# Two row buffers in an expert loop, the last tile's rows added by a product, and three smaller reorderings, in a two-layer backbone

## The chip, the cores and the metric

One Trainium2 chip, one of its cores. The metric is the device time of one execution of the program, in microseconds (us). The kernel before was timed in three runs.

## The reference, cut to what matters

Two layers run over 256 latent tokens and 256 context tokens of width 1024. Each layer mixes tokens (a state space branch, a gated branch, differential attention, sigmoid gates, one output projection) and then sends every token through 8 of 64 experts and one shared expert. All is float32. In the last layer only the latent tokens go through the experts.

```python
# differential attention, per head: two score matrices, m = 0 and 1
s = einsum('bqhmd,bkhmd->bhmqk', q, k) * DA_HEAD_DIM ** -0.5
p = softmax(s); attn = p[:, :, 0] - lam * p[:, :, 1]
...
out = m @ w_out                                    # the out product of the mixer
h = layer_norm(DN_ALPHA * h + g1 * out, ln1_g, ln1_b)
f = modulate(layer_norm(h), sh2, sc2)
...
# experts: each token's rows through its 8 experts, weighted, summed over the experts
yb = swiglu(h_pad[tok], w_gate[e], w_up[e], w_down[e]) * wt[:, None]
y = segment_sum(yb, row_tok) + swiglu(h, w_sh_gate, w_sh_up, w_sh_down)
h = layer_norm(DN_ALPHA * h + g2 * y, ln2_g, ln2_b)
```

## The kernel before, in words

Outside the expert stage a list scheduler orders the instructions of each engine, with a cost model; `self.urgent`, `self.hold`, `background` and `paced` are hints to it. Inside `experts` (from line 1521) the order is written by hand.

**Expert stage.** The (token, expert) pairs are sorted by expert into tiles of 128 rows, made of four groups of 32 rows, each with one expert. The groups belong to three lanes, `LANE_OF = (0, 0, 1, 2)`, so that a token appears at most once per lane and tile; each lane has an accumulator in DRAM, `acc`, of one row of 1024 numbers per token. Layer 0 has 38 tiles and layer 1 has 20; the first 32 and 16 are always run, the rest stand in nested conditions (`rest`, line 1684). One step `body(t)` issues, in this order: the gate and up products of tile t (`gate_up`, line 1630, 64 records on the product engine); the last weight copies of the tile; the activation; the transposes of tile t+1's gathered rows (`x_t`); the weight copies of tile t+1 from the ring of loaded weights (`copy_gu`, line 1578, lanes 0 and 2 on DVE, lane 1 on ACT; `copy_dn`, line 1584, DVE); the transposes of the hidden rows; POOL's indirect gather of tile t+2's rows (line 1554); and then `down(t-1)`: the down products (line 1646), ACT's two copies of the result, scaled by the routing weight, to the row buffer `Y` (line 1648), with two of ACT's weight copies in between, and POOL's indirect DMA that adds the rows of `Y` to `acc` (the scatter, line 1651).

`Y` is one buffer of 128 x 1024 numbers, so ACT writes tile t's rows once the scatter of tile t-1 has landed. Two scatters add to the same `acc`, so POOL starts one when the one before has landed. ACT runs its instructions in order: what waits for `Y` holds up the weight copies behind it, for which `gate_up` waits. On POOL a gather stands behind the scatter issued before it. SP loads the experts' weights, three times 1 MB each, to a ring of four slots (`load_next`), when DVE's and ACT's copies have freed a slot.

**Combine** (from line 1711). After the last scatter, g2 and the gain and bias of the norm are spread from one row to 128 partitions by products with a row of ones (lines 1719 to 1726) and used from PSUM (the bias is copied to SBUF). Per token tile (four in layer 0, two in layer 1) SP loads the three lanes of `acc` (line 1742); they are added by DVE for the first tile and by POOL for the others (line 1745); DVE multiplies by g2 (line 1746) and adds the scaled residual (line 1748); `ln_two` normalises (DVE, ACT, POOL); SP writes the tile out (line 1752). In layer 0 the next layer's `mixer_input` (lines 330 to 371) follows directly: transposes on the product engine (line 366), then the input projection.

**Attention** (line 731 and on). Per token tile and head, for m = 0 and then m = 1: a score product over 64 rows of the array (line 737), the maximum on DVE (line 740), the exponential on ACT. The two m use different halves of the rows and different PSUM banks.

**Out product, layer 1.** Two token tiles (2 and 3), two halves of 512 columns. The weights of half 1 are prepared ahead by `out_weights`; those of half 0 are loaded and split within a loop over k, which runs tile 2's two halves and tile 3's first half; tile 3's second half follows. Then `residual` (lines 997 to 1000) loads a half of the residual input `op_h` on SP and adds it, `ln_two` runs twice per tile, and the router's products and a sigmoid (line 1042) follow.

The program is made in `kernel` with the default space for the descriptors of indirect DMAs.

## Time and profile before

| | us |
|---|---|
| runs before, median of 3 (lowest to highest) | 2016.36 (2011.74 to 2021.05) |
| the profiled execution, its own time | 2016.54 |
| its span, first to last instruction | 2014.5 |
| around the span | 2.0 |
| mean granted clock of the product engine, share of full speed | 0.921 |

Engines are PE (products; PEld its weight loads), DVE, ACT, POOL and SP (which issues loads); a "q" behind a name is an engine's instruction queue. In a row of the timeline stand the start, the busy time, the engine, the line of the kernel, the operation, what it writes and reads, how many instructions were merged, and in brackets how long the engine stood idle before it and what ended that. A row of the waits says which instruction waited for which, for how long in all, how often, and the longest. [...] Busy shares are averages over stages that have different limits.

### The profile page before, as it was taken

How to read it: one execution, taken by the hardware profiler on the slowest of the kernel's cores; microseconds unless marked ns; L12 is line 12 of the kernel's file. 1: busy time of each engine (PE TensorE's matmuls, PEld its weight loads, DVE VectorE, ACT ScalarE, POOL GpSimd, SP SyncE). 2: the span in 40 equal slices, each digit the busy share in tenths (PEclk: the TensorE clock that was granted, in tenths of full speed). 3: DMA queues.
4: the chain of work that ended last, by engine and by line, in shares of the span. 5: the costliest groups of instructions: out<-in, count | busy, mean ns of one | idle time of the engine just before them, and what ended most of it. 6: DMA issues, size and time to landing. Idle time of an engine off the chain costs nothing. (4 is left out here: it accounts for less than half of the span.)

```text
span 2014.5 us, 33549 instructions
## 1 busy us (share of the span) xinstructions
PE 1724.2 (86%) x12397; PEld 1009.1 (50%) x12397; DVE 1153.1 (57%) x2295; ACT 792.6 (39%) x1317; POOL 585.0 (29%) x385
## 2 busy tenths in 40 slices
PE   5898999999997988999889763889989689897883
PEld 2686866778865323333323221777779653232231
DVE  7688554333654756766565546663554456655554
ACT  3344343323313544555444343432454224443441
POOL 5355310222201324343233224323042202331222
PEclk8898999999998989999999885889999789998996
DMA  8113524553767555677798937635564567999974
GB/s 273 48 48 116 170 95 139 182 191 134 265 240 309 171 187 182 220 220 242 263 354 313 360 90 269 215 130 183 187 194 130 206 245 275 323 343 354 386 263 122
DMA packets 158391, 435.02 MB, mean 216 GB/s; under 512 B 25813, under 2 KB 82547, under 8 KB 133114
## 3 DMA queue, kind: packets, MB, share of 16 engines
q1 hardware_dynamic: 124716, 344.04, 46.5%
q0 software_dynamic: 17280, 51.93, 10.7%
q10 hardware_dynamic: 16206, 36.66, 5.0%
q8 instruction: 103, 1.69, 0.3%
q14 instruction: 86, 0.70, 0.1%
HBM read 403.16 MB, written 55.03 MB: 227 GB/s over the span
## 5 line engine op out<-in xcount | busy, mean ns | idle before, releaser
L1630 PE MATMUL pg<-gu,xt 128*32 128x512 f32 x3712 | 487.4, 641 | 105.0 <-ACT gu L1578 65.8
L1578 DVE COPY gu<-raw 128x1024 f32 x476 | 298.8, 689 | 160.0 <-issue 82.1
L1651 POOL DMA_INDIRECT acc<-y,t_scatter x58 | 208.8, 3600 | 584.0 <-ACT y L1648 313.1
L1630 PEld LDWEIGHTS pg<-gu,xt 128*32 128x32 f32 x3712 | 141.1, 117 | 438.9 <-issue 238.8
L1578 ACT COPY gu<-raw 128x1024 f32 x238 | 244.3, 1043 | 63.2 <-PE pg L1630 35.7
L1646 PE MATMUL py<-dn,ht 128*32 128x512 f32 x1856 | 211.1, 595 | 2.5 <-ACT gu L1578 1.7
L1584 DVE COPY dn<-raw 128x2048 f32 x178 | 212.9, 1224 | 0.4 <-issue 0.4
L136 PE MATMUL mm<-uh,whi 128*128 128x512 f32 (+1 forms) x544 | 199.3, 366 | 7.9 <-ACT rx L849 4.5
L138 PE MATMUL mm<-uh,wlo 128*128 128x512 f32 (+1 forms) x544 | 194.8, 358 | 0.5 <-DVE wlo L315 0.5
L137 PE MATMUL mm<-ul,whi 128*128 128x512 f32 (+1 forms) x544 | 194.2, 357 | 0.0
L315 DVE TENSOR_TENSOR wlo<-raw,whi 128x1024 fp32r<-128x1024 f32 x77 | 97.0, 1261 | 110.6 <-ACT whi L312 110.2
L312 ACT CAST whi<-raw 128x1024 fp32r<-128x1024 f32 x92 | 96.1, 1047 | 145.3 <-PE mm L137 121.3
L1648 ACT ACTIVATE y<-py,w 128x512 f32<-128x512 f32 x116 | 79.7, 689 | 157.0 <-DMA acc<-y,t_scatter 147.5
L1635 DVE TENSOR_TENSOR sg<-sg,pg 128x256 f32<-128x256 f32 x58 | 24.4, 421 | 195.7 <-ACT sg L1634 195.7
L136 PEld LDWEIGHTS mm<-uh,whi 128*128 128x128 f32 x544 | 106.3, 195 | 33.5 <-issue 8.0
L1634 ACT ACTIVATE sg<-pg 128x256 f32<-128x256 f32 x58 | 22.3, 384 | 250.1 <-PE pg L1630 250.1
L137 PEld LDWEIGHTS mm<-ul,whi 128*128 128x128 f32 x544 | 106.3, 195 | 17.1 <-issue 4.6
L1554 POOL DMA_INDIRECT xg<-f,t_gather x62 | 67.3, 1085 | 162.8 <-DVE t_scatter L1518 68.2
L138 PEld LDWEIGHTS mm<-uh,wlo 128*128 128x128 f32 x544 | 106.1, 195 | 16.1 <-issue 2.3
L1646 PEld LDWEIGHTS py<-dn,ht 128*32 128x32 f32 x1856 | 54.6, 109 | 114.9 <-issue 107.9
L1622 PEld LDWEIGHTS px<-ct,xg 128*128 128x128 f32 x480 | 58.8, 194 | 60.1 <-issue 60.1
L1622 PE MATMUL px<-ct,xg 128*128 128x128 f32 x480 | 70.4, 290 | 9.9 <-DMA xg<-f,t_gather 9.9
(482 smaller groups left out, 2823.1 us busy)
## 6 DMA issues: line engine op xcount, KB each, us to landing
raw<-in_w_exp_gate_dram SPq DMA_DIRECT2D x68, 1024.0 KB
raw<-in_w_exp_up_dram SPq DMA_DIRECT2D x68, 1024.0 KB
raw<-in_w_exp_down_dram SPq DMA_DIRECT2D x68, 1024.0 KB
raw<-in_w_in_dram SPq DMA_DIRECT2D x42, 1024.0 KB
mraw<-in_w_mod_dram SPq DMA_DIRECT2D x80, 512.0 KB
cb_y<-acc SPq DMA_DIRECT2D x18, 512.0 KB
fraw<-in_w_mod_dram SPq DMA_DIRECT2D x16, 512.0 KB
acc<-zt ACTq DMA_DIRECT2D x12, 512.0 KB
```

Of the source, the lines that this page charges most:

```text
L136: nc.tensor.matmul(out, lh, rh, start=start, stop=False)
L137: nc.tensor.matmul(out, lh, rl, start=False, stop=False)
L138: self.last = nc.tensor.matmul(out, ll, rh, start=False, stop=stop).ins
L312: self.nc.scalar.copy(hv, src)
L315: i = eng.tensor_tensor(lv, src, hv.bitcast(F32), op=ALU.subtract)
L1578: c = nc.scalar.copy(dst, gu) if ln == 1 else V.tensor_copy(dst, gu)
L1584: c = V.tensor_copy(DN[ln][t % 2].rearrange("p a b -> p (a b)"), srcs[ln][:, 4096:6144])
L1622: nc.tensor.transpose(pX[hf][:, k * P:(k + 1) * P], XG[t % AHEAD][:, 4 * hf + k:D:8], ident)
L1630: nc.tensor.matmul(pG[t % 2][r, :], XT[:, k, r], GU[ln][(4 * t + k // 2) % 3][:, k % 2].rearrange("p g n -> p (g n)"), start=(k == 0), sto ...
L1646: nc.tensor.matmul(pY[hf][r, :], HT[t % 2][:, k, r], DN[ln][t % 2][:, k, 512 * hf:512 * hf + 512], start=(k == 0), stop=(k == 1), tile_pos ...
L1648: nc.scalar.activation(Y[:, 512 * hf:512 * hf + 512], pY[hf], AF.Copy, scale=W[t % 4])
L1651: nc.gpsimd.indirect_dma_start(out=acc, out_offset=bass.IndirectOffsetOnAxis(ap=tb["scatter"][:, t:t + 1], axis=0), in_=Y, in_offset=None, ...
```

## The change

The last expert tile's rows go to a buffer that stays (`self.yl`), with their token numbers (`self.il`); no scatter follows. In `combine` they are added by a product with a 0/1 matrix (token number of the row equal to the column's), accumulated in PSUM with the three lanes, each multiplied by the identity. So the sums of lanes are eight products per token tile, and DVE reads the sum from PSUM. The spread rows are copied to SBUF by ACT, those of the norm after the first tile's products; all tiles of h are loaded at the start. `Y` has two buffers. The space for descriptors of indirect DMAs is set to 8192, half of before. In attention both score products of a head are issued ahead of both maxima. In layer 1 the out product has both halves' weights prepared ahead, runs by tile (tile 2's halves, then tile 3's), the residual input is loaded whole and early, and a sigmoid of one column is issued ahead of the first tile's norm.

```diff
 # attention
-                for m in range(2):
+                both = [pp.tile([P, 512], F32, name="att", tag="att", bufs=2) for m in range(2)]
+                for m, ps in enumerate(both):
                     r = slice(64 * m, 64 * m + 64)
-                    ps = pp.tile([P, 512], F32, name="att", tag="att", bufs=2)
                     qk = nc.tensor.matmul(ps[:, :nk], ...)
+                for m, ps in enumerate(both):
                     mx = pool.tile([P, 1], F32, name="mx", bufs=4)
...
 # out_first
+            if l == DEPTH - 1:
+                half["h"][t] = pool.tile([P, D], F32, name="op_h%d" % t)
+                self.nc.sync.dma_start(half["h"][t], h_tiles[t])
 # out_proj
+            if l == DEPTH - 1 and t == tiles[0]:
+                nc.scalar.activation(pool.tile([P, 1], F32, name="op_sg"), half["sm"][t][:, 0:1], AF.Sigmoid)
 # mixer
+                if not full:
+                    w0 = [ow.tile([P, KC, 512], F32R, name="wn%d" % i) for i in range(2)]
+                    self.out_weights(l, 0, self.mod_raw, *w0)
                 self.out_weights(l, 1, self.mod_raw, *w1)
...
+                for t in tiles if not full else ():
+                    c = slice(t * P - t0, t * P - t0 + P)
+                    for p, w, hf in ((ps[t], w0, 0), (ps1[t], w1, 1)):
+                        self.out_half(p, mh, ml, *w, c.start)
+                        if hf == 0:
+                            self.residual(op, half, t, 0, p, h_tiles[t])
-                for k in range(KC):
+                for k in range(KC) if full else ():
...
 # experts
-            Y = pool.tile([P, D], F32, name="y")
+            Y = [pool.tile([P, D], F32, name="y%d" % i) for i in range(2)]
...
-            def down(t, between=()):
+            def down(t, between=(), last=False):
+                y = self.yl if last else Y[t % 2]
...
-                    nc.scalar.activation(Y[:, 512 * hf:512 * hf + 512], pY[hf], AF.Copy, scale=W[t % 4])
+                    nc.scalar.activation(y[:, 512 * hf:512 * hf + 512], pY[hf], AF.Copy, scale=W[t % 4])
...
+                if last:
+                    V.tensor_copy(self.il, tb["gather"][:, t:t + 1])
+                    return
                 nc.gpsimd.indirect_dma_start(out=acc, ..., in_=y, ..., compute_op=ALU.add)
...
-                        down(t - 1)
+                        down(t - 1, last=True)
...
 # combine
-                return ps
+                v = pool.tile([P, D], F32, name="cb_" + name)
+                nc.scalar.copy(v, ps)
+                return v
...
-            for t in range(2):
+            for t in range(len(streams)):
                 nc.sync.dma_start(tiles[t], h1_tiles[t])
...
-                ys = [pool.tile([P, D], F32, name="cb_y%d" % i, bufs=4 if i < 2 else 2) for i in range(LANES)]
+                ys = [pool.tile([P, D], F32, name="cb_y%d" % i, bufs=3) for i in range(LANES)]
...
-                for a in ys[1:]:
-                    (G if t else V).tensor_tensor(y, y, a, op=ALU.add)
-                V.tensor_mul(y, y, g2[s])
+                if s not in g2:
+                    g2[s] = spread(self.modD[l][s:s + 1, 3 * D:4 * D], "g2_%d" % s)
+                oh = pool.tile([P, P], F32, name="cb_oh", bufs=2)
+                V.tensor_scalar(oh, self.C("iota"), float(t * P), self.il, op0=ALU.add, op1=ALU.is_equal)
+                yp = pp.tile([P, D], F32, name="cb_yp", bufs=2)
+                for i in range(0, D, 512):
+                    for j, (a, w) in enumerate([(self.yl, oh)] + [(a, self.C("ident")) for a in ys]):
+                        nc.tensor.matmul(yp[:, i:i + 512], w, a[:, i:i + 512], start=(j == 0), stop=(j == LANES))
+                if t == 0:
+                    lg, lb = (spread(A[nm][l:l + 1, :], nm) for nm in ("ln2_g", "ln2_b"))
+                y = ys[0]
+                V.tensor_mul(y, yp, g2[s])
...
 # kernel
-    nc = _bacc.Bacc("TRN2", target_bir_lowering=False, num_devices=1)
+    nc = _bacc.Bacc("TRN2", target_bir_lowering=False, num_devices=1, dynamic_dma_scratch_size=8192)
```

## Rows read from the trace of the kernel before

**Rows 1.** The page's part 1: engine, busy us (share of the span) and instructions.
```profile
PE 1724.2 (86%) x12397; PEld 1009.1 (50%) x12397; DVE 1153.1 (57%) x2295; ACT 792.6 (39%) x1317; POOL 585.0 (29%) x385
```

**Rows 2.** The waits, whole span: who waited for whom, us in total, times, longest.
```profile
POOL acc L1651 <- DVE gu L1578: 229.8, 22, 17.3
...
ACT y L1648 <- DMA acc<-y,t_scatter: 147.5, 33, 8.7
```

**Rows 3.** Timeline of PE, a tile that nothing holds.
```profile
867.16 7.05 PE L1630 MATMUL pg<-gu,xt 128*32 128x512 f32 x64
...
879.06 7.05 PE L1630 MATMUL pg<-gu,xt 128*32 128x512 f32 x64
```

**Rows 4.** Timeline of POOL and ACT, a held tile, layer 0.
```profile
692.54 6.03 POOL L1651 DMA_INDIRECT acc<-y,t_scatter  x1 [7.74 <-DVE gu L1578]
...
708.51 0.69 ACT L1648 ACTIVATE y<-py,w 128x512 f32<-128x512 f32 x1 [6.92 <-DMA acc<-y,t_scatter]
...
711.00 1.59 POOL L1651 DMA_INDIRECT acc<-y,t_scatter  x1 [11.08 <-ACT y L1648]
712.89 1.04 POOL L1554 DMA_INDIRECT xg<-f,t_gather  x1 [0.30 <-issue]
```

**Rows 5.** Line 1648's idle time (us, times) in 660 to 880, 880 to 1140, 1680 to 1830.
```profile
  DMA acc<-y,t_scatter: 30.2, 8
...
  DMA acc<-y,t_scatter: 49.3, 11
...
  DMA acc<-y,t_scatter: 32.7, 7
```

**Rows 6.** Stretches: length, busy time by engine, granted clock, DMA share, GB/s.
```profile
667.00:872.00 205.00, 187.82 (x1528) 66.60 (x1523) 129.29 (x201) 99.48 (x143) 77.58 (x30) 0.95 0.64 206
872.00:1132.00 260.00, 232.37 (x1892) 81.51 (x1886) 157.99 (x249) 122.59 (x178) 83.12 (x35) 0.96 0.82 290
...
1204.00:1266.00 62.00, 22.23 (x44) 9.76 (x44) 38.58 (x61) 20.61 (x30) 28.47 (x20) 0.50 0.70 247
...
1686.00:1821.00 135.00, 118.31 (x970) 41.67 (x966) 84.64 (x131) 62.02 (x91) 44.02 (x19) 0.96 0.90 324
...
1860.00:1940.00 80.00, 64.63 (x506) 21.46 (x498) 40.13 (x63) 34.01 (x49) 19.68 (x10) 0.96 1.01 390
```

**Rows 7.** Tile acc, all its 58 scatters and the accumulator loads: time to landing.
```profile
DMA to landing us min/median/max: 5.9/10.7/16.3
```

**Rows 8.** Tile xg, its 62 gathers: time to landing.
```profile
DMA to landing us min/median/max: 4.4/10.2/13.1
```

**Rows 9.** Timeline of all engines at the end of layer 0.
```profile
1206.46 1.27 ACT L1648 ACTIVATE y<-py,w 128x512 f32<-128x512 f32 x2 [8.74 <-DMA acc<-y,t_scatter]
...
1210.61 7.19 PE L1725 MATMUL g<-g,cb_one 1*128 1x512 f32 x8 [11.37 <-POOL cb_one L1717]
...
1216.60 15.28 SPq L1742 DMA_DIRECT2D cb_y<-acc  x12
...
1222.07 2.48 DVE L1745 TENSOR_TENSOR cb_y<-cb_y,cb_y 128x1024 f32<-128x1024 f32 x2 [22.70 <-DMA cb_y<-acc]
...
1225.92 3.40 DVE L1748 SCALAR_TENSOR_TENSOR cb_h<-cb_h,cb_y 128x1024 f32<-128x1024 f32 x1
```

**Rows 10.** Timeline of ACT at the end of layer 1.
```profile
1976.81 1.27 ACT L1648 ACTIVATE y<-py,w 128x512 f32<-128x512 f32 x2 [7.25 <-DMA acc<-y,t_scatter]
```

**Rows 11.** Timeline of PE, DVE and ACT behind layer 1's out product.
```profile
1584.27 0.39 PE L138 MATMUL opp<-whi,mh 128*128 128x512 f32 x1
...
1591.31 0.69 DVE L1000 SCALAR_TENSOR_TENSOR op_r<-op_h,op_r 128x512 f32<-128x512 f32 x1 [3.47 <-DMA op_h<-h]
...
1606.03 1.28 ACT L1042 ACT_TABLE_LOAD   x1 [2.05 <-DVE op_f L189]
```

**Rows 12.** Timeline of PE, score products of layer 1, apart and together.
```profile
1390.34 1.12 PE L737 MATMUL att<-kT,qT 64*128 64x512 f32 x2
...
1395.54 1.13 PE L737 MATMUL att<-kT,qT 64*128 64x512 f32 x4
```

More of the change, by code (lines that the diff above doesn't have):

```diff
@@ L111, in __init__ @@
         self.eps = self.per.tile([P, 3], F32, name="eps")
+        self.yl = self.per.tile([P, D], F32, name="yl")
+        self.il = self.per.tile([P, 1], F32, name="il")
         self.hpi = self.eps[:, 2:3]
@@ L980, in shared_expert, with out_first @@
             yield
-    def out_first(self, l, pool, tiles):
-        half = dict(r={}, sm={}, g={})
+    def out_first(self, l, pool, tiles, h_tiles):
+        half = dict(r={}, sm={}, g={}, h={})
         for s in sorted(set(t // 2 for t in tiles)):
@@ L995, in residual @@
         c = slice(512 * hf, 512 * hf + 512)
-        h = pool.tile([P, 512], F32, name="op_h", bufs=2 if self.l < DEPTH - 1 else 4)
-        self.nc.sync.dma_start(h, h_tile[:, c])
+        if t in half["h"]:
+            h = half["h"][t][:, c]
+        else:
+            h = pool.tile([P, 512], F32, name="op_h", bufs=2)
+            self.nc.sync.dma_start(h, h_tile[:, c])
         r = half["r"][t][:, c]
@@ L1150, in mixer @@
                 op = pool("opr", hx, side="right")
-                half = self.out_first(l, op, tiles)
+                half = self.out_first(l, op, tiles, h_tiles)
                 ow = pool("opw", hx, side="right")
                 w1 = [ow.tile([P, KC, 512], F32R, name="wo%d" % i) for i in range(2)]
+                if not full:
+                    w0 = [ow.tile([P, KC, 512], F32R, name="wn%d" % i) for i in range(2)]
+                    self.out_weights(l, 0, self.mod_raw, *w0)
                 self.out_weights(l, 1, self.mod_raw, *w1)
@@ L1167, in mixer @@
                         self.mm3(ps[t], mh[:, k, c], ml[:, k, c], hv[:, k % 2, :], lv[:, k % 2, :], k == 0, k == KC - 1)
-                        if t == 2 and not full:
-                            self.mm3(ps1[t], mh[:, k, c], ml[:, k, c], w1[0][:, k, :], w1[1][:, k, :], k == 0, k == KC - 1)
-                if not full:
-                    self.out_half(ps1[3], mh, ml, *w1, 3 * P - t0)
-                for t in tiles:
+                for t in tiles if full else ():
                     self.residual(op, half, t, 0, ps[t], h_tiles[t])
@@ L1689, in rest @@
                     with more.Else():
-                        down(t - 1)
+                        down(t - 1, last=True)
                 else:
-                    down(t - 1)
+                    down(t - 1, last=True)
             for t in range(AHEAD):
@@ L1719, in spread @@
             def spread(row, name):
[L1721 removed]
+                v = pool.tile([1, D], F32, name="cb_row", bufs=2)
                 nc.scalar.dma_start(v, row)
[L1723 removed]
+                ps = pp.tile([P, D], F32, name="cb_ps", bufs=2)
                 for i in range(0, D, 512):
                     nc.tensor.matmul(ps[:, i:i + 512], one, v[:, i:i + 512], start=True, stop=True)
[L1726 to L1730 removed]
+                v = pool.tile([P, D], F32, name="cb_" + name)
+                nc.scalar.copy(v, ps)
+                return v
+            g2 = {}
             tiles = [pool.tile([P, D], F32, name="cb_h%d" % t) for t in range(len(streams))]
[L1732 removed]
+            for t in range(len(streams)):
                 nc.sync.dma_start(tiles[t], h1_tiles[t])
```

11 lines of the change are left out of this document (1 added, 10 removed).

## The prediction

> **What bounds the kernel now.** I read the page first, then the waits, then one tile of the expert stage in order of time, then the stages. The page gives the product engine 1724.2 us, 86% of the span [rows 1]. The remaining 290 us are idle time, and after idle time the engine also runs slowly, so the question is which wait holds it up in the expert stages. In the list of waits, two entries belong to one loop: ACT waited 147.5 us, 33 times, for the landing of a scatter before it could write the next y, and POOL's scatter started late behind DVE's weight copies, 229.8 us in 22 waits [rows 2]. The loop exists because y is one buffer: y(t) can't be written until scatter(t-1) has read it and landed.
>
> Two tiles show what the loop costs. A tile that nothing holds takes 879.06 - 867.16 = 11.9 us from one gate/up start to the next [rows 3]. In a held one [rows 4] a scatter issued at 692.54 occupied POOL for 6.03 us, and landed just ahead of 708.51, 16 us after issue. ACT sat 6.92 us, and the weight copies for which gate/up waits stood behind it. The next scatter came at 711.00, 18.46 us after the first: 6.56 us over 11.9, for 6.92 us of waiting. So a wait of y costs the tile 0.95 of its length, partly hidden, and partly paid again in slow products behind the gap.
>
> By stretch, y waited 30.2, 49.3 and 32.7 us [rows 5] (layer 0 early, layer 0 late, layer 1 early; 16, 18 and 10 tiles, at two copies of y each). The other 35.3 us of the 147.5 lie in tiles that wait for weight loads anyway, and in the two last tiles. The loads' own share of the DMA engines was 0.64, 0.82 and 0.90 in these stretches, and 1.01 where loads bind, late in layer 1 [rows 6].
>
> **The row buffers.** With Y in two buffers, y(t) waits for scatter(t-2). Times 0.95 the three stretches could give back 28.7, 46.8 and 31.0 us, which is the upper bound, 106. Two things take from it. First, scatter(t) still waits on POOL for scatter(t-1)'s landing, since both add into one accumulator. Landings took 5.9 / 10.7 / 16.3 us (min, median, max) [rows 7]. Spread evenly over the upper half, 0.39 of the tiles lie above 11.9, by 2.2 us on the mean: 0.87 us a tile is kept. Second, the same bytes must be loaded in less time; at a share of 0.94 (between 0.90 and 1.01) the stretches of 205, 260 and 135 us can't fall below 140, 227 and 129, a gain of at most 33 in the second and 6 in the third, or 13 at a share of 1.0.
> - Early layer 0, 16 tiles: 28.7 - 14 = 15.
> - Late layer 0, 18 tiles: 46.8 - 15.7 = 31, under the limit of 33.
> - Early layer 1, 10 tiles: 31 - 8.7 = 22, limited to 6 to 13, say 9.
> - The late tiles: 0.
>
> The sum is **-55**. With no tile kept and loads at 1.0 it is 28.7 + 46.8 + 13 = -88. If every scatter comes in the upper half (middle 13.5, so 1.6 kept a tile), it is 3 + 18 + 9 = -30. Behind a waiting scatter POOL's next gather is queued. Its landing takes 10.2 us at the median [rows 8] and it is wanted about 11.9 + 7.05 us after y is written, so a scatter that is up to about 6 us late hides it; I count nothing, and a rival counts it.
>
> The scatter's length has a cause in the rows. It is 6.03 us on POOL beside DVE's copies and 1.59 us once they are done [rows 4]. [...]
>
> **Layer 0's end.** The last y waits 8.74 us for the scatter before it; then comes its own scatter, and the accumulator loads issue at 1216.60 [rows 9]. Without the last scatter they can issue when the last y starts now, at 1206.46: 10.1 us earlier. Against that stand the sums by products. [...] I take 9.5 for the first tile, slow at first, less the 2.48 us of DVE adds that go [rows 9]: -10.1 + 9.5 - 2.5 = -3. The three other tiles' products lie beside the normalisation of the tile before, as POOL's adds do now; the scaled add drops from 3.40 us beside those adds [rows 9], so another -2: **-5**. [...] The spreads' copies on ACT and the early loads of h lie beside the wait for the accumulators.
>
> **Layer 1's end.** The last y waits 7.25 us [rows 10], the path is the same and the gain again 10.1. Only two token tiles follow, and nothing after them: -3 for the first, and for the second 7 us of products where about 5 us of the first's normalisation cover, +2: **-1**. [...]
>
> About the clock, the trace shows 0.50 through both the wait and the spreads, from 1204 to 1266 [rows 6]. [...]
>
> **Layer 1's out product.** The last product starts at 1584.27, but a residual half waits until 1591.31 for its load of h, 3.47 us of it idle [rows 11]; a table load of 1.28 us stands ahead of the router's sigmoid. With h loaded early and tile 2 finished half the products sooner, only tile 3's chain is left behind the last product. I take 3.5 for the load, 1.3 for the table and 3 for tile 2's instructions that no longer stand in tile 3's way: **-8** (0 to -11). The extra weights' loads replace as many bytes; their cover is the stage's earlier products.
>
> **Paired scores.** Two score products apart take 1.12 us for two records each; four records together take 1.13 [rows 12]. I counted all 24 pairs: 16 run apart now, so at most 16 x 1 = 16 us; but the engine has other work there while DVE takes the maxima, and order changes elsewhere: **-4** (0 to -15).
>
> **Half the descriptor space:** 0. A scatter at 711.00 and a gather at 712.89 are in flight together [rows 4]; half the space holds at least one.
>
> The sum is -55 - 5 - 1 - 8 - 4 = -73. The profiled execution took 2016.5 us (span 2014.5, 2.0 around it), the median of the runs is 2016.4, so no correction: **1943**.
>
> **Rivals.**
> 1. *Scatters in a chain.* Every scatter takes the long form, and the loop runs at its landing. For it: 22 waits behind DVE [rows 2]. Against: the median of 10.7 is below 11.9. The gain is 30 in place of 55: 1968.
> 2. *Tiles at 11.9 until loads bind.* For it: a gather and a scatter cost nothing in an unheld tile. -88: 1943 - 33 = 1910.
> [...]
> 4. *A gather queued behind a waiting scatter* comes late by what y no longer waits, so the expert stages gain nothing: 1998. It decides once a scatter issues over about 6 us late in two tiles running.
> 5. *Slower: the halved descriptor space holds only one indirect DMA.* Then scatter and gather wait for each other's landing, 10.7 + 10.2 = 20.9 us a tile where I expect 12.8: 58 x 8.1 = 470 us, 2413. It decides as soon as one scatter with one gather exceeds the half; against it is only that the whole holds both.
>
> **Numbers.** My forecast has 0.45, the rivals 0.17, 0.12, 0.12, 0.08 and 0.03, and other losses 0.03. The range reaches from below rival 2 to above rival 3, **1902 to 1990**. A measurement of this kernel can tell about 0.5%, 10 us. Faster: the first four cases and a quarter of rival 4, 0.88. Same: the rest of it, 0.06. Slower: 0.06.
>
> **What would show it.** Right: ACT's wait for the scatter falls from 147.5 to under 50 us, in its place POOL waits for landings; tiles run near 12.8; the accumulator loads issue about 10 us after the last down product's predecessor landed, not 20; the granted clock rises within the sums. [...] The prediction is wrong if the expert stages gain under 30 us or over 88.

## The result, and where the time went

The changed kernel takes 1982.78 us (median of 4 runs, 1978.30 to 1985.32) beside 2015.56 us for the kernel before on the same chip (4 runs, 2011.74 to 2021.05): a ratio of 0.9833, interval [0.9803, 0.9862]. It is faster by 1.7%, and inside the range, but by 33 us where 73 were forecast. The span fell from 2014.5 to 1980.1 us, by 34.4. Ratios here and below are of fast runs; one slow run of E14, at 3302 us, is not in its ratio.

Both traces are cut at the same landmarks (the first gate/up product, the last down product, the first and last score product of layer 1, the last out product, the router's transposes), with the two best experiments beside them. Lengths in us:

| stage | before | changed | difference | E1: rows alone | E10: best |
|---|---|---|---|---|---|
| start to first gate/up product | 641.7 | 646.8 | +5.1 | 647.7 | 647.7 |
| experts, layer 0, to the end of the last down product | 557.5 | 509.6 | **-47.9** | 508.3 | 516.6 |
| layer 0's combine and layer 1's projection, to the first score product | 191.1 | 201.1 | **+10.0** | 173.5 | 172.9 |
| attention, layer 1 | 72.3 | 71.2 | -1.1 | 72.4 | 72.5 |
| last score product to last out product | 121.7 | 134.9 | **+13.2** | 121.7 | 121.5 |
| to the last router transpose | 23.1 | 18.7 | -4.4 | 23.0 | 19.5 |
| to layer 1's first gate/up product | 49.1 | 48.3 | -0.8 | 47.7 | 48.6 |
| experts, layer 1 | 315.2 | 304.6 | **-10.6** | 303.5 | 303.3 |
| combine, layer 1 | 42.8 | 44.9 | +2.1 | 38.0 | 38.2 |
| span | 2014.5 | 1980.1 | -34.4 | 1935.9 | 1940.9 |

So the expert stages gained 58.5 us, and other stages gave 24 of it back. Stages with the same work in them tell how far one profile can be trusted: the first, where only the paired scores and the use of SBUF differ, lies between 641.7 and 648.2 in the runs below, and layer 0's expert stage between 508.3 and 519.0 in those with two row buffers.

The page's part 1 of the changed kernel answers to [rows 1]; the product engine is busier in a shorter span, and POOL less busy:

```profile
PE 1750.4 (88%) x12493; PEld 1026.8 (52%) x12493; DVE 1149.7 (58%) x2300; ACT 803.3 (41%) x1327; POOL 542.0 (27%) x378
```

**The expert stages.** The waits of the changed kernel (who waited for whom, us in total, times, longest) answer to [rows 2]:

```profile
POOL acc L1674 <- DVE gu L1597: 254.0, 26, 17.4
...
POOL acc L1674 <- DMA acc<-y,t_scatter: 63.4, 7, 9.6
...
PEld px L1641 <- DMA xg<-f,t_gather: 36.0, 19, 3.6
...
DVE cb_y L1775 <- PE cb_yp L1771: 28.6, 4, 24.8
```

ACT's wait for the scatter, 147.5 us before, is in the list no more. POOL waits 63.4 us for landings in its place, as the prediction said, and 254.0 behind DVE, but ACT isn't queued behind POOL. The windows of the same stages (length, busy time of PE, PEld, DVE, ACT, POOL, granted clock, DMA share, GB/s), and below them three short ones for later, answer to [rows 6]:

```profile
647.00:847.00 200.00, 193.98 (x1664) 72.03 (x1664) 141.64 (x220) 110.71 (x158) 74.09 (x30) 1.00 0.69 219
847.00:1068.00 221.00, 208.29 (x1806) 75.71 (x1798) 152.78 (x238) 120.48 (x173) 68.56 (x34) 0.99 0.90 314
1631.00:1764.00 133.00, 121.64 (x1036) 45.43 (x1032) 89.80 (x142) 69.30 (x99) 37.66 (x18) 0.97 0.89 333
1764.00:1918.00 154.00, 123.50 (x954) 43.63 (x950) 81.16 (x127) 63.28 (x90) 30.12 (x18) 0.91 0.96 362
...
1160.79:1177.85 17.06, 15.15 (x17) 5.34 (x18) 0.00 (x0) 2.02 (x2) 0.19 (x1) 0.50 0.92 363
...
1939.02:1956.09 17.07, 14.51 (x16) 5.01 (x17) 0.00 (x0) 2.02 (x2) 0.19 (x1) 0.50 0.59 226
...
1528.00:1564.00 36.00, 27.35 (x96) 20.53 (x96) 16.04 (x18) 10.22 (x18) 11.18 (x8) 0.81 0.59 223
```

The first 16 tiles of layer 0 take 12.5 us each (14.1 before), the next 17 take 13.0 (14.2), the first 10 of layer 1 13.3 (14.5); the last 9, where weight loads bind (a DMA share of 0.96 in the fourth window), are no shorter (154.5 us for 152.6). PE works 97% of the first window, and the loads' share rose to 0.90 in the second.

**Layer 0's combine.** The timeline of all engines (start, busy time, what it does, in brackets the idle time before it and its end) answers to [rows 9]:

```profile
1161.00 21.42 SPq L1761 DMA_DIRECT2D cb_y<-acc  x11
...
1162.70 3.75 PE L1748 MATMUL cb_ps<-cb_row,cb_one 1*128 1x512 f32 x4 [6.27 <-DMA cb_row<-modD]
...
1166.38 2.08 PE L1771 MATMUL cb_yp<-yl,cb_oh 128*128 128x512 f32 x2
...
1168.38 3.78 PE L1748 MATMUL cb_ps<-cb_row,cb_one 1*128 1x512 f32 x4
...
1173.96 4.68 PE L1771 MATMUL cb_yp<-cb_y,ct 128*128 128x512 f32 x6
...
1182.16 1.22 DVE L1775 TENSOR_TENSOR cb_y<-cb_yp,cb_g 128x1024 f32<-128x1024 f32 x1 [2.34 <-PE cb_yp L1771]
```

The loads now issue 4.6 us after the last down product, 17.4 before: 12.8 earlier, more than the 10.1 forecast. But from the first load to the first multiplication by g2 it is 21.2 us where it was 8.1; in layer 1 it is 20.0 for 8.8. The lanes' products stand behind the spreads (that of the norm's gain too, which the code has behind them and the scheduler puts first), and from 1160.79 to 1177.85 all of it runs at a granted clock of 0.50 (the fifth window above; the sixth is layer 1's). The combine grew by 5.6 us, from 67.4 to 73.0 between the last down product and layer 1's first input product, and the projection behind it by 4.3, from 123.7 to 128.0.

**Layer 1's out product.** The timeline of PE and ACT answers to [rows 11]:

```profile
1527.79 2.18 ACT L939 CAST wn<-mraw 128x512 fp32r<-128x512 f32 x4
...
1528.46 0.74 PE L139 MATMUL opp<-wn,mh 128*128 128x512 f32 x2 [2.42 <-ACT wn L939]
...
1543.33 2.42 ACT L939 CAST wn<-mraw 128x512 fp32r<-128x512 f32 x4 [13.36 <-DMA mraw<-in_w_out_dram]
1544.00 1.22 PE L139 MATMUL opp<-wn,mh 128*128 128x512 f32 x2 [7.43 <-ACT wn L939]
```

The first weights are split (written as a rounded part, by ACT, and the rest) at the moment they are wanted. Before, the splits of the weights made ahead stood 40 to 50 us ahead of the first product at 1536.4 (number, ns of one, first and last start):

```profile
L935 ACT CAST wo<-mraw x8: 612/616/621, 1486.8 to 1496.8; 128x512 fp32r<-128x512 f32 x8
```

The stretch runs at a clock of 0.81 (the last window above).

### The profile page after: what moved, and what is told of

Its sections match the earlier page's. It is cut to its first block, busy times and chain, and to the rows that moved or that the text cites. A ratio compares the mean times of both kernels' runs of the same rounds, so it can differ in the third digit from the quotient of the medians.

```text
span 1980.1 us, 33726 instructions
## 1 busy us (share of the span) xinstructions
PE 1750.4 (88%) x12493; PEld 1026.8 (52%) x12493; DVE 1149.7 (58%) x2300; ACT 803.3 (41%) x1327; POOL 542.0 (27%) x378
## 3 DMA queue, kind: packets, MB, share of 16 engines
q0 software_dynamic: 16992, 51.66, 10.7%
## 5 line engine op out<-in xcount | busy, mean ns | idle before, releaser
L1649 PE MATMUL pg<-gu,xt 128*32 128x512 f32 x3712 | 454.8, 616 | 56.6 <-DVE gu L1597 45.1
L1674 POOL DMA_INDIRECT acc<-y,t_scatter x56 | 173.5, 3099 | 534.6 <-DVE gu L1597 254.0
L315 ACT CAST whi<-raw 128x1024 fp32r<-128x1024 f32 x88 | 91.8, 1047 | 142.6 <-PE mm L140 122.2
L1573 POOL DMA_INDIRECT xg<-f,t_gather x62 | 72.7, 1173 | 161.1 <-DVE t_scatter L1537 109.3
L140 PEld LDWEIGHTS mm<-ul,whi 128*128 128x128 f32 x544 | 106.8, 196 | 17.4 <-issue 4.5
L149 POOL TENSOR_TENSOR rs_r<-rs_ve,eps 128x1 f32<-128x1 f32 (+1 forms) x38 | 37.8, 996 | 223.5 <-DVE rs_ve L147 200.6
```

What stands on the lines that cost most here:

```text
L140: nc.tensor.matmul(out, lh, rl, start=False, stop=False)
L315: self.nc.scalar.copy(hv, src)
L1649: nc.tensor.matmul(pG[t % 2][r, :], XT[:, k, r], GU[ln][(4 * t + k // 2) % 3][:, k % 2].rearrange("p g n -> p (g n)"), start=(k == 0), sto ...
L1674: nc.gpsimd.indirect_dma_start(out=acc, out_offset=bass.IndirectOffsetOnAxis(ap=tb["scatter"][:, t:t + 1], axis=0), in_=y, in_offset=None, ...
```

## The experiments

My theory then: the row buffers are worth about what was forecast; the out product by tile and the sums by products each cost where a gain was counted. Rivals were that the rows gain less and the rest is noise, or that the last tile's product, and not the lanes', is the cost. Where E4, E6, E7, E8 and E11 to E13 start from the changed kernel, the diff is against it. Intervals are for the ratio to the kernel before.

**E1, the rows alone.** The kernel before with two row buffers and half the descriptor space.

```diff
-            Y = pool.tile([P, D], F32, name="y")
+            Y = [pool.tile([P, D], F32, name="y%d" % i) for i in range(2)]
...
-                                             in_=Y, in_offset=None, ..., compute_op=ALU.add)
+                                             in_=Y[t % 2], in_offset=None, ..., compute_op=ALU.add)
...
+    nc = _bacc.Bacc(..., dynamic_dma_scratch_size=8192)
```

> The kernel before with two row buffers and the halved descriptor space, nothing else. Theory (the expert stages gained what was forecast and other parts gave it back): the expert stages shorten by 48 us in layer 0 and 10 us in layer 1 as in the changed kernel, the rest is as before: 2015.6 - 58 = about 1958 us, 25 us faster than the whole change. Rival (the row buffers gain little by themselves, and the last tile's product and the order of the rest made part of it): 1980 or more.

Measured: 1939.83 us, 0.9624 [0.958, 0.9667], better than the whole change and better than expected. Its expert stages take 811.8 us, the changed kernel's 814.2, before 872.7 (from the table). Two gains beyond them were in no forecast. The last y of each layer waits no more for the scatter before it (8.74 and 7.25 us before, [rows 9, 10]), so both combines are shorter, by 5.0 us in layer 0 (62.4 for 67.4 to the first input product) and 4.7 in layer 1; and layer 1's projection is shorter, 111.1 us for 123.7 (E5). Two row buffers without the halved space were not run.

**E2, one row buffer** in the changed kernel.

```diff
-            Y = [pool.tile([P, D], F32, name="y%d" % i) for i in range(2)]
+            Y = pool.tile([P, D], F32, name="y")
...
-                y = self.yl if last else Y[t % 2]
+                y = self.yl if last else Y
```

> The changed kernel with one row buffer. Theory: ACT's wait for the scatter returns (about 140 us in the list of waits), the expert stages are as long as before, and the time is 1983 + 58 = about 2041 us, slower than before by the 25 us that the other parts cost. Rival (the other parts gain too): 2016 or less.

Measured: 2050.98 us, 1.0145 [1.0103, 1.0188]; the expert stages take 878.5 us, about as long as before. So the row buffers are worth 63 to 68 us in this kernel (by the ratios, and by the medians), and the rest of the change costs about 30 us against the kernel before.

**E3, the out product as before**, early h and early sigmoid kept.

```diff
-                if not full:
-                    w0 = [ow.tile([P, KC, 512], F32R, name="wn%d" % i) for i in range(2)]
-                    self.out_weights(l, 0, self.mod_raw, *w0)
...
-                for t in tiles if not full else ():
...
-                for k in range(KC) if full else ():
+                for k in range(KC):
...
+                        if t == 2 and not full:
+                            self.mm3(ps1[t], mh[:, k, c], ml[:, k, c], w1[0][:, k, :], w1[1][:, k, :], k == 0, k == KC - 1)
+                if not full:
+                    self.out_half(ps1[3], mh, ml, *w1, 3 * P - t0)
```

> The changed kernel with layer 1's out product in the loop over k of before (half 0's weights split in the loop); the whole early load of h and the early sigmoid stay. Theory (the product waits for weights that are prepared too late, 2.4 and 7.4 us of gap and slow products behind it): the stretch from the last score product to the last out product falls from 134.9 to about 120 us, with the early h another 4 us behind it stay gained: 1983 - 13 = about 1970 us. Rival (the stretch is longer because of work that moved there from elsewhere): 1980 to 1985.

Measured: 1967.18 us, 0.975 [0.9716, 0.9784]. The stretch to the last out product falls from 134.9 to 119.7 us: that product costs about 15 us against the loop it replaced.

**E4, the lanes added by DVE and POOL** as before, only the last tile's rows put there by a product.

```diff
-  for j, (a, w) in enumerate([(self.yl, oh)] + [(a, self.C("ident")) for a in ys]):
-      nc.tensor.matmul(yp[:, i:i + 512], w, a[:, i:i + 512], ...)
+  nc.tensor.matmul(yp[:, i:i + 512], oh, self.yl[:, i:i + 512], start=True, stop=True)
...
-  V.tensor_mul(y, yp, g2[s])
+  for a in ys[1:]: (G if t else V).tensor_tensor(y, y, a, op=ALU.add)
+  V.tensor_add(y, y, yp)
+  V.tensor_mul(y, y, g2[s])
```

> The changed kernel with the lanes summed by DVE and POOL adds as before; the last tile's rows still come by a product, added by one more DVE operation per token tile. Theory (32 and 16 records a lane sum less on the product engine, which is what ends last behind both expert stages): the first multiply comes about 10 us after the first accumulator load and not 21, layer 0's end is 7 to 12 us shorter and layer 1's 6 to 9: 1983 - 16 = about 1967 us. Rival (the spreads and the norm's chain set these ends, not the products): 1980 to 1986.

Measured: 1977.18 us, 0.9784 [0.9738, 0.983]; layer 1's combine 37.3 us for 44.9 (42.4 to 44.0 in the five other runs with two row buffers and these sums), but layer 0's stage only 2.4 shorter (198.7 for 201.1). By the medians this is a third of what was expected; the intervals of the two kernels overlap, so the gain is shown in layer 1's combine and not in the total. Its timeline in layer 1 shows what the lanes' products cost:

```profile
1940.64 3.67 SPq L1761 DMA_DIRECT2D cb_y<-acc  x6
...
1946.83 1.23 DVE L1775 TENSOR_TENSOR cb_y<-cb_y,cb_y 128x1024 f32<-128x1024 f32 x1 [9.79 <-DMA cb_y<-acc]
...
1950.97 5.62 POOL L1775 TENSOR_TENSOR cb_y<-cb_y,cb_y 128x1024 f32<-128x1024 f32 x2 [9.33 <-DMA cb_y<-acc]
1951.00 3.39 DVE L1777 TENSOR_TENSOR cb_y<-cb_y,cb_g 128x1024 f32<-128x1024 f32 x1
```

The lanes have landed 6.2 us after the first load, and the first multiplication starts 10.4 after it, not 20.0. Some of it goes again: that multiplication takes 3.39 us beside POOL's add, and 1.22 in the changed kernel.

**E5, half the descriptor space alone**, in the kernel before.

```diff
-    nc = _bacc.Bacc("TRN2", target_bir_lowering=False, num_devices=1)
+    nc = _bacc.Bacc("TRN2", target_bir_lowering=False, num_devices=1, dynamic_dma_scratch_size=8192)
```

> The kernel before with the halved descriptor space alone. Two row buffers with the halved space gave 20 us more than the expert stages can account for, most of it in layer 1's projection (99.4 us from its first product to the first score product, against 123.7 before and 127.2 in the changed kernel). Theory (the space that is freed in SBUF lets the scheduler put input products where the engine waited for the gated branch's transposes, so the clock no longer falls there): the order of the products in that stretch is that of the run with two row buffers, the stretch takes about 100 us, and the time is 2016 - 15 = about 2000 us, with the expert stages as before. Rival (the stretch is shorter because of the row buffers, through the state in which the stage starts): 2014 to 2018.

Measured: 2001.97 us beside 2013.69, 0.9937 [0.9904, 0.997]. A term that I had put at 0 gains 13 us (12 by the medians). The expert stages, where the indirect DMAs run, take 872.3 us together, as before (one 6.6 longer, the other 7.1 shorter); the gain lies between layer 0's last down product and layer 1's first score product (176.2 us for 191.1). PE's work has another order there. In the timeline of PE before, it stands idle for the gated branch's transposes:

```profile
1335.74 0.77 PE L803 MATMUL tr<-ct,yb 128*128 128x128 f32 x2 [4.86 <-DVE yb L800]
```

and the granted clock is 0.50 from 1333.62 on, for 17.07 us (before):

```profile
1333.62:1350.69 17.07, 14.26 (x52) 12.68 (x53) 4.60 (x15) 4.00 (x9) 2.08 (x3) 0.50 0.58 192
```

In E5 input products stand between the transposes, and the same wait is shorter:

```profile
1326.98 0.31 PE L803 MATMUL tr<-ct,yb 128*128 128x128 f32 x1
1327.05 0.48 PE L137 MATMUL mm<-ul,whi 128*128 128x512 f32 x1
...
1339.50 0.30 PE L803 MATMUL tr<-ct,yb 128*128 128x128 f32 x1 [1.47 <-DVE yb L800]
```

By its code the scheduler issues an instruction when there is room for its output; that the halved space leaves more room in SBUF, and that it puts the input products earlier for that reason, was my estimate. The trace shows the order alone.

**E6, `yl` later.** The changed kernel has the halved space too, and yet its projection is not shorter. Its `yl` takes 4 KB from the start; here it is allocated only ahead of the expert stage.

```diff
-        self.yl = self.per.tile([P, D], F32, name="yl")
+            yp = pool("ylp", keep, side="right")
+            self.yl, self.il = yp.tile([P, D], F32, name="yl"), yp.tile([P, 1], F32, name="il")
```

> The changed kernel, whole, with the last tile's row buffer (4 KB in each partition) and its token numbers allocated just ahead of the expert stage and not at the start of the program. Theory (that buffer takes the room in the mixer that the halved descriptor space had freed, and with it the better order of layer 1's projection): the projection stretch takes about 100 us and not 127, and the time is 1983 - 18 = about 1965 us. Rival (the long stretch comes from the sums by products or from the paired scores ahead of it): 1978 to 1988.

Measured: 1973.38 us, 0.9786 [0.9732, 0.984], an interval that overlaps the changed kernel's; the stage takes 187.4 us for 201.1, and 6 us of that are lost again between the out product and layer 1's experts (73.1 for 67.0), for which I have no cause. The windows from the first input product to the first score product, of the kernel before, E1, the changed kernel and E6, in this order (columns as above), show that it is partly the clock: 0.88 and 0.97 for the same 775 records, 0.88 and 0.97 for the same 810. (The 99.4 us for E1 in E5's expectation, and the 100 in E6's, are counted from 11.6 us behind its first input product.)

```profile
1266.64:1390.34 123.70, 110.98 (x775) 90.46 (x775) 65.50 (x126) 40.26 (x67) 42.08 (x40) 0.88 0.52 171
```

```profile
1218.39:1329.51 111.12, 102.71 (x775) 83.07 (x775) 66.43 (x126) 40.36 (x67) 41.24 (x40) 0.97 0.57 186
```

```profile
1229.46:1357.50 128.04, 116.25 (x811) 93.30 (x811) 65.04 (x126) 40.92 (x69) 42.39 (x39) 0.88 0.54 176
```

```profile
1231.24:1345.07 113.83, 106.88 (x810) 85.43 (x810) 65.09 (x126) 40.95 (x69) 40.08 (x39) 0.97 0.59 194
```

All runs fall in line: this stretch takes 110.5 to 113.8 us in the seven with the halved space and no `yl` in the mixer (E1, E5, E6, E8, E9, E10, E14), and 127.5 to 129.4 in the changed kernel and the seven that have `yl` from the start.

**E7, no spreads and an engine kept busy.** In the changed kernel the rows of g2 and the norm are broadcast by DMA in place of the products, and 13 products without use follow each last down product.

```diff
+                    for i in range(13):
+                        nc.tensor.matmul(pX[i % 2], ident, XT[:, 0:4, :]..., start=True, stop=True)
...
-                v = pool.tile([1, D], F32, name="cb_row", bufs=2)
+                v = pool.tile([P, D], F32, name="cb_" + name)
                 nc.scalar.dma_start(v, row)
...
-                    nc.tensor.matmul(ps[:, i:i + 512], one, v[:, i:i + 512], start=True, stop=True)
...
-                nc.scalar.copy(v, ps)
...
-                    g2[s] = spread(self.modD[l][s:s + 1, 3 * D:4 * D], "g2_%d" % s)
+                    g2[s] = spread(self.bcast(self.modD[l][s, 3 * D:4 * D], D), "g2_%d" % s)
```

> [...] Rival (the landing of the lanes and the norm's chain set the ends): 1978 or more.

Measured: 1981.77 us, 0.9837 [0.9782, 0.9892], no gain in all; my estimate was 1966 us, with the clock at 1.00 until the sums and the first multiplication 13 us after the first load. At layer 1's end the clock did what the edit was for; the window and the timeline:

```profile
1915.86:1973.89 58.03, 50.94 (x272) 19.21 (x264) 25.56 (x42) 16.66 (x25) 11.20 (x5) 1.00 0.41 133
```

```profile
1946.99 6.52 SPq L1758 DMA_DIRECT2D cb_y<-acc  x6
...
1954.87 1.12 PE L1768 MATMUL cb_yp<-cb_y,ct 128*128 128x512 f32 x2 [0.25 <-DMA cb_y<-acc]
1957.11 2.38 PE L1768 MATMUL cb_yp<-cb_y,ct 128*128 128x512 f32 x4 [1.11 <-DMA cb_y<-acc]
...
1962.96 1.23 DVE L1772 TENSOR_TENSOR cb_y<-cb_yp,cb_g 128x1024 f32<-128x1024 f32 x1 [20.11 <-PE cb_yp L1768]
```

The clock stays at 1.00, the lanes' products wait for nothing but landings, and the combine takes 39.3 us for 44.9. The first multiplication starts 16.0 us after the first load, 20.0 in the changed kernel and 8.8 before. So of the 11.2 us lost, the spreads and the low clock hold 4; the rest is the later landing and the products at a clock of 1.00. (The broadcast DMAs run beside the loads here; that they delay the landing isn't shown.) In layer 0 the last down products ended later (23.0 us from the last gate/up product's start, for 17.0) and the loads issued 7.9 us after them for 4.6, which took the gain back; I didn't follow up why.

**E11, half 1's weights first**, the products half by half, in the changed kernel: was it the order of the two loads that made the first half late?

```diff
+                self.out_weights(l, 1, self.mod_raw, *w1)
                 if not full:
...
-                self.out_weights(l, 1, self.mod_raw, *w1)
...
+                for w, hf, acc_ps in ((w1, 1, ps1), (w0, 0, ps)) if not full else ():
+                    for t in tiles:
+                        self.out_half(acc_ps[t], mh, ml, *w, t * P - t0)
```

> The changed kernel with half 1's weights of layer 1's out product prepared first and its products of both tiles ahead of half 0's. Theory (half 1's buffer lies where it lay before and is free early, half 0's lies where the mixer's data are until the last gate; the changed kernel prepares half 0 first, and half 1 queues behind it for the two load buffers): half 1's casts run about 40 us ahead of the first out product, as before, and the out product has at most one short gap: 1983 - 9 = about 1974 us. Rival (both halves' room is free only behind the last gate, or the scheduler puts both off): the casts come within 5 us of the first out product and the time is 1980 or more.

Measured: 1984.12 us, 0.9818 [0.9767, 0.987]; the splits begin at 1528.65, as before the edit. That theory fell: whichever half comes first is split only behind the last gate.

**E13, room of its own for half 0.** The changed kernel's "opw" holds both halves, 64 KB per partition, of which part is room that the gates hold to their end. Here half 0 has a pool of 32 KB for itself, opened first.

```diff
                 if not full:
+                    ow = pool("opw0", hx, side="right")
                     w0 = [ow.tile([P, KC, 512], F32R, name="wn%d" % i) for i in range(2)]
                     self.out_weights(l, 0, self.mod_raw, *w0)
+                ow = pool("opw", hx, side="right")
+                w1 = [ow.tile([P, KC, 512], F32R, name="wo%d" % i) for i in range(2)]
                 self.out_weights(l, 1, self.mod_raw, *w1)
...
+                for w, hf, acc_ps in ((w0, 0, ps), (w1, 1, ps1)) if not full else ():
+                    for t in tiles:
+                        self.out_half(acc_ps[t], mh, ml, *w, t * P - t0)
```

> The changed kernel with the weights of the out projection's first column half given room of their own, apart from the second half's, and the products taken half by half (first half for both tiles, then the second). Theory (room): the first half is split only behind the last gate since its room overlaps what the gates still hold; with room of its own its splits stand tens of us ahead of the first out product, the two gaps (2.42 and 7.43 us before the products at 1528 and 1544 us) go, the stretch from attention's last product to the last out product falls from 134.9 to 120 to 125 us, and the time by 10 to 13 us, to about 1971 us. Rival (order): the splits stand behind the gates on ScalarE because the order of its work puts them there, room or not; then the stretch stays at 130 to 135 us and the time within 4 us of 1982.

Measured: 1982.77 us, 0.9817 [0.9796, 0.9837]. The mechanism is the theory's, the total the rival's. By the view of one tile (ns of one, first and last start) half 0 is split from 1452.3 on and its products start at 1500.2, 70.7 us after attention and not 99.7:

```profile
L939 ACT CAST wn<-mraw x8: 612/620/624, 1452.3 to 1462.9; 128x512 fp32r<-128x512 f32 x8
```

```profile
L139 PE MATMUL opp<-wn,mh x16: 393/393/501, 1500.2 to 1536.7; 128*128 128x512 f32 x16
```

The wait then moved to half 1. ACT's rows of E13, and PE's:

```profile
1535.70 0.41 ACT L134 CAST mh<-gt 128x256 fp32r<-128x256 f32 x1 [2.36 <-POOL gt L926]
1536.65 2.18 ACT L939 CAST wo<-mraw 128x512 fp32r<-128x512 f32 x4 [0.55 <-DVE mh L135]
1551.69 2.42 ACT L939 CAST wo<-mraw 128x512 fp32r<-128x512 f32 x4 [10.38 <-DMA mraw<-in_w_out_dram]
```

```profile
1552.36 1.22 PE L139 MATMUL opp<-wo,mh 128*128 128x512 f32 x2 [7.85 <-ACT wo L939]
```

Half 1's splits start right behind the last gate's cast (its first two loads had been issued at 1461.94 and 1464.95); its second two loads could be issued only when the first had been split, since there are two raw buffers. The stretch is 130.3 us for 134.9.

**E14, the same edit in the best version** (E10 below), in place of its loop over k.

> The kernel of two row buffers, early pre-norm rows and paired scores with the sums of before (1939 us), and in it the out product of layer 1 half by half with the first half's weights in room of their own. Its k-outermost products already start with the weights there (attention's last product to the last out product about 120 us), so by either theory the products themselves cost the same; what can be won is that the first half's residual starts while the second half's products run: 0 to 5 us, 1934 to 1940 us. If the weights come late here too, as in the changed kernel, it is slower by 8 to 15 us, 1947 to 1954 us.

Measured: 1947.88 us, 0.9656 [0.9626, 0.9686], 8 us slower than E10 (14 by the ratios): here too half 1's product waits 9.08 us for its weights, and the stretch is 134.6 us for 121.5. So in these runs one half of the weights was split beside the gates, the second only behind them. By the code, the loop of before needs no second half ahead, and moves along k as the gates deliver.

**E12, scores apart** in the changed kernel; **E9**, E1 with early h and early sigmoid; **E10**, E9 with paired scores. E9's edit, and E10's (E12 takes it back):

```diff
+            if l == DEPTH - 1:
+                half["h"][t] = pool.tile([P, D], F32, name="op_h%d" % t)
+                self.nc.sync.dma_start(half["h"][t], h_tiles[t])
...
+            if l == DEPTH - 1 and t == tiles[0]:
+                nc.scalar.activation(pool.tile([P, 1], F32, name="op_sg"), half["sm"][t][:, 0:1], AF.Sigmoid)
```

```diff
-                for m in range(2):
+                both = [pp.tile([P, 512], F32, name="att", tag="att", bufs=2) for m in range(2)]
+                for m, ps in enumerate(both):
...
+                for m, ps in enumerate(both):
```

> The changed kernel with the scores in the order of before. Theory: no difference, 1981 to 1985. Rival (pairing costs the 5 us by which the changed kernel reaches its first expert tile later than the kernel before): about 1978, first gate/up at 642 us. Other rival (pairing gains): 1987 or more.

> The run with two row buffers and the halved space, and of the other parts only the whole early load of h and the early sigmoid in layer 1 (out product, sums and scores as before). Theory (these two shorten what follows the out product by 3.6 to 4.4 us, as in the changed kernel, and touch nothing else): 1940 - 4 = about 1936 us. Rival (they change the scheduler's order elsewhere): 1945 or more.

> The run before it in this list, with the paired scores. Theory (the engine is busy all through the attention stages, 133.6 of 134.5 us, so a pair that runs together only frees time that other products had filled): the same to 2 us. Rival (the forecast's 4 us, up to 15): 4 us or more faster.

Measured: E12 1984.60 us, 0.9827 [0.9782, 0.9872]; E9 1943.05, 0.9612 [0.957, 0.9654]; E10 1939.42, 0.9587 [0.9543, 0.9632]. Layer 0's attention takes 136.4 us paired (the changed kernel) and apart (E12), 136.4 and 136.5 in E10 and E9, and layer 1's 71.2 and 71.2: pairing is worth nothing that shows. Early h and sigmoid cut the stretch to the last router transpose by 3.5 us (19.5 in E10 for 23.0 in E1); E9's total shows nothing of it. E10 beats both kernels; from E1, whose interval overlaps, it can't be told apart.

**E8, the change mended**: `yl` later, the out product and the lanes' adds as before (E3, E4 and E6 together).

> A mend: the changed kernel with the last tile's row buffer allocated just ahead of the expert stage, layer 1's out product in the loop of before (early h and early sigmoid kept), and the lanes summed by adds, only the last tile's rows by a product. Theory: the run with two row buffers alone (1940) less about 3.6 us behind the out product, with the ends about as there: 1933 to 1940 us. Rival (the parts don't add up, since each moves the order of the others): 1945 or more.

Measured: 1948.80 us, 0.9681 [0.9633, 0.973], slower than expected, as its rival said. Layer 1's combine is the shortest of all at 34.2 us, 3.8 below E1's, so the last tile's product does win there once the lanes are added as before; but layer 0's combine and projection take 187.8 us for E1's 173.5. All of this lies in the combine: layer 1's first input product comes 77.2 us after the last down product, in E1 62.4, and from there it is 110.6 us to the first score product, in E1 111.1. The timeline shows where:

```profile
1193.00 1.21 DVE L1769 TENSOR_TENSOR cb_y<-cb_y,cb_yp 128x1024 f32<-128x1024 f32 x1
...
1202.11 0.99 ACT L1743 COPY cb_g<-cb_ps 128x1024 f32<-128x1024 f32 x1
...
1205.26 1.21 DVE L1770 TENSOR_TENSOR cb_y<-cb_y,cb_g 128x1024 f32<-128x1024 f32 x1
```

The third token tile's sum is whole at 1194.2, but its multiplication needs the second stream's g2, which ACT copies to SBUF only at 1202.11, behind steps of the normalisation and two weight casts; in E1, where g2 is used from PSUM, that multiplication starts 38.4 us after the last down product and not 49.1. In E4 the copy stands at 1202.13, and the multiplication comes 43.5 us after. No run moved this copy alone, so that it is the whole of the loss is argued.

## Why the prediction was wrong

- **The row buffers: right in the mechanism, and the sum in part by luck.** -58.5 us for the forecast -55, and 12.5, 13.0 and 13.3 us a tile. Of the three stretches, the first gave 25.3 (15 forecast), the second 21.1 (31), layer 1's 12.4 (9): one error of 10 us made up for another. In the first I had kept 0.87 us a tile for scatters that land late, and cut the gain of 28.7 to 15; PE was idle there for 6 us of 200, so little of it was paid. In the second the loads' share reached 0.90, where I had let it go to 0.94, and the tiles stayed above the 12.8 of the forecast. (The stretches of 205 and 135 us by which the forecast limits the loads hold 14 and 9 tiles, not 16 and 10; those took 225.5 and 145.3. The limits move by under 1 us.)
- **The scatter's length.** A scatter is long beside DVE's copies (6.03 us for 1.59, [rows 4]), and rival 1 had every one of them long, for -30. That did not come about: 22 of 58 took over 5 us before, 14 of 56 after. In the profile's costliest groups (count | busy us, mean ns | idle us ahead of them and what ended most of it) the mean scatter fell from 3.60 us, before, to 3.10, after, though POOL's wait behind DVE rose from 229.8 to 254.0 us:

```profile
L1651 POOL DMA_INDIRECT acc<-y,t_scatter x58 | 208.8, 3600 | 584.0 <-ACT y L1648 313.1
```

```profile
L1674 POOL DMA_INDIRECT acc<-y,t_scatter x56 | 173.5, 3099 | 534.6 <-DVE gu L1597 254.0
```

- **Both combines: the step that failed** is "9.5 for the first tile, less the 2.48 us of DVE adds". That counted the products at their length, as if they could start with the landing. In the rows the lanes' products stand behind eight spread records and the last tile's own four, 11.3 us from 1162.70 to 1173.96, and run at a clock of 0.50 themselves until 1177.85. Adds on DVE wait for landings alone (8.1 and 8.8 us before). With the earlier loads the stretch from the last down product to the first multiplication is 25.7 us for 25.4 in layer 0 and 25.5 for 23.6 in layer 1: the whole gain of the missing scatter is spent. Layer 1's combine is at +2.1 (forecast -1; -0.4 to +1.3 in the five other runs with these sums), and E4 shows there that the lanes' products are the cost: with adds it is 37.3 us. Layer 0's stage is at +10 (forecast -5), 5.6 of it in the combine and 4.3 in the projection, which go with `yl` (E6); E4 wins only 2.4 in this stage, so what the products cost in it stays open. The prediction also had the spreads' copies beside the wait for the accumulators: in the changed kernel DVE waits 1.91 us for one of them (the norm's bias, at 1189.41), and in E4 and E8 the third tile stands behind another. It also missed that two row buffers alone win 5 us at either end, since the last y needn't wait: the last scatter's removal was credited with a wait that the other part removes.
- **The clock.** No run shows the 9.5 us for the first tile's sum at either end; it was an estimate of mine from the 7.19 us that eight records took at 0.50 [rows 6, 9]. In the changed kernel the first tile's records in layer 0 lie between 1166.38 and 1182.16, spreads among them: 15.8 us at a mean clock of 0.64. The 7 us for the second tile in layer 1, an estimate too, E7 shows at 1.00: its sixteen records lie between 1962.76 and 1969.79. In the changed kernel the clock was 0.50 for 17.06 us of the spreads and sums, with the engine 15.15 us busy in them; in E7, behind products without use, it was 1.00 throughout at layer 1's end. But the low clock holds only a part of the loss: E7 without it is still at 16.0 us for 8.8. The slow products behind a gap that the prediction speaks of stand in the held tile of [rows 4], in the kernel before; 44 records behind 4.27 us of idling took 8.12 us, at a mean clock of 0.65, where 64 take 7.05 when nothing holds them [rows 3]:

```profile
710.18 8.12 PE L1630 MATMUL pg<-gu,xt 128*32 128x512 f32 x44 [4.27 <-ACT gu L1578]
```

- **Layer 1's out product: the step that failed** is "the extra weights' loads replace as many bytes; their cover is the stage's earlier products". The loads of the first two chunks were issued in good time, at 1430.35; what was missing was room for the split weights until the gates' end (E13), and raw buffers to refill. The stretch cost 13.2 us, and the loop of before takes 15.2 off again (E3). The other pieces were right in kind: h, sigmoid and tile 2's chain gave 4.4 of the 7.8 counted.
- **Paired scores:** 0 for -4; at the low end of its bounds.
- **Half the descriptor space:** put at 0. In the changed kernel nothing of it shows, but by accident: alone the space gains 13 us, and `yl` takes the gain in that stage back (14.9 us in E5, 13.7 in E6). That room in SBUF is how it does so was my estimate; E6 fits it, no trace shows it. No rival had a change of SBUF use reorder a stage without an edit.

Of the rivals, none took place as stated. Rival 3, in the range and in the chances, stands for both ends at a clock of 0.50 throughout, by an estimate from the 7.19 us for eight records [rows 9] +26 us in place of -6, so 1975. It was nearest, for part of its cause: the clock was 0.50 for 17.06 and 17.07 us there, and 1.00 from then until the first multiplication. The forecast's own bounds for the expert stages (30 to 88 us) held, ACT's wait went and POOL's came, the loads issued earlier and the clock rose within the sums; the 39 us between forecast and span were lost at the out product (17), layer 0's combine with the projection (15), ahead of the expert stage (5, as in E1 and the other runs), at the scores (4) and layer 1's combine (3), against some 5 more than counted elsewhere.

## What to carry to other kernels

Work that moves to an idle engine must be priced with what stands ahead of it in that engine's order and with the clock granted there (0.50 for 17 us at both ends here); a sum that waits only for its landing on another engine can be the faster one, however idle the product engine looks (layer 1's combine takes 37.3 us with adds in E4, for 44.9). When an operand is made ahead, ask what room it is made in and who holds that room: a load issued 97 us ahead of its split is worth nothing if its split has to wait. And where a scheduler places work by free room, 4 KB of SBUF can move a stage that the diff doesn't touch (`yl`, 13.7 us in E6), so test each part alone: here two parts of six, the row buffers and the halved space, gained 76 us by themselves (E1), and the whole change 33.

## What the runs showed of the hardware that I had not expected

- At both ends the clock stayed at 0.50 for 17 us while PE was busy for 15.15 and 14.51 us of them, in spreads and sums without long gaps.
- The same 810 records of layer 1's projection take 128.0 us at a mean clock of 0.88 and 113.8 at 0.97, with PE idle for 11.8 and 7.0 us; where small waits fall goes with both.
- Half the space for descriptors (8192) held scatters and gathers with no loss that shows: the landings of `acc` go from 5.9 / 10.7 / 16.3 us [rows 7] to 6.7 / 11.5 / 15.6, the gathers' from 4.4 / 10.2 / 13.1 [rows 8] to 5.0 / 10.3 / 13.2.
